# Moving tiles in SBUF, and reusing the meta tokens' keys, in a two-request encoder layer on one Trainium2 core

## The chip, the cores and the metric

The kernel runs on one core of a Trainium2 chip, on TensorE (PE), VectorE (DVE), ScalarE (ACT), GpSimd (POOL) and SyncE (SP), which issues most DMAs. The metric is the device time of the one launch in microseconds. A run's time is the median of several executions; the profile is one further execution, and its span runs from the first to the last instruction.

## What is computed

One layer of an encoder is applied to two requests that share weights: a "prompt" of 1024 tokens and a "sample" of 512, both float32, width 1024. Cut to what matters here:

```python
def encoder_layer(x, ...):                       # x: (1, 16 + T, 1024), 16 meta tokens first
    h = rmsnorm(x, g_mix)
    q, k, v, u, gate_na, gate_fn = split(h @ w_in)
    y_na = neighbourhood_attention(q, k, v, rel_bias, meta_bias) @ w_branch_na
    y_fn = fourier_mix(u) @ w_branch_fn          # real part of a 2-D DFT over positions and channels
    x = x + (sigmoid(gate_na) * y_na + sigmoid(gate_fn) * y_fn) @ w_out
    a = relu(rmsnorm(x, g_mlp) @ w_up)
    return x + (a * a) @ w_down

def run_trunk(x, meta_tokens, ...):
    h = concatenate([meta_tokens, x])            # the same 16 rows ahead of either request
    return rmsnorm(encoder_layer(h, ...), g_final)[16:]
```

Each token of a grid 64 wide attends to a window of 8 x 16 neighbours and to the 16 meta tokens. The meta tokens' own keys, values and normalized rows depend on nothing but themselves and the weights, so they are equal in both requests. The Fourier mix runs over all 16 + T positions.

## The kernel before

The sample runs first, then the prompt (`run`, L330). Each goes through the same stages: reading and transposing the normalized tokens into `hT` (L262), values (L291), attention with the K and Q projections inside (L474), the gates (L736) with the folding of positions beside them (L823), the merges, the Fourier stage (L909), the output projection, and the MLP. In the prompt the MLP's up and down products are done by a Strassen scheme (class `Halves`, L1156; up at L1417).

Every product is kept near float32 by three products of float32r halves: an operand is split into a rounded part `hi` (a CAST on ACT, L151 or L132) and the rest `lo` (a subtraction on DVE or POOL, L152 or L133), and `mm3` (L121; the matmul is L128) issues hi x hi, hi x lo and lo x hi. Most matmuls contract 128 rows and write 128 x 512. The K and Q projections have their own matmul lines (L491 to L493).

`hT` is a pair of tiles (hi, lo) of shape [128, 8, T + 16]: eight blocks of 128 channels, each a row of T + 16 positions with the 16 meta positions first (`new_hT`, L471). A row of the sample is 528 floats, one of the prompt 1040. Weights rotate through three names of tiles of 1044 floats, `w_raw`, `w_hi`, `w_lo`, two buffers each (`wtile`, L135).

The keys of two heads at a time are made in chunks of columns (L479): 352, 344 and 344 in the prompt, 264 and 264 in the sample. The first chunk begins with the 16 meta positions, whose keys ACT and DVE copy six times into the first and last "slot" of the tile `k` (L528 to L534); POOL first zeroes gaps there (L516, `k<-zero`). From the second pair of heads on, POOL also sends half of `k` to the other 64 partitions by DMA (L537). POOL prepares the mask tiles `bm` too (L727, L734).

`fold_positions` (L823) uses a symmetry of the DFT: it adds and subtracts position p and its mirror. For each of the eight blocks a step adds hi and lo of both halves (L839, into `a` and `b`), and makes sum and difference (L840 to L842); a second series of eight steps splits the results back into `hT`. In the sample `a` is the tile `gain`, of which there is one buffer (L380), and the kept halves lie in `acc` and `hn` tiles. The eight first steps run beside the gates, pinned behind their products. Beside the same gates `fold_u` (L236) multiplies the channel DFT into weights (PE L246), evicts them through ACT and DVE (L132, L133, as `w_hi` and `w_lo`), and stores them by SP (L254, L255); POOL's queue loads them later (L819). `tables` (L200) builds the bias tables of attention in DRAM at the start of the sample.

Within an engine's queue the instructions run in order; the order comes from the scheduler of the tile framework and from the `behind` and `pinned` contexts (L110, L114). A tile's buffer is written again only after all its readers, DMAs among them, are done.

Of the kernel before, what the change touches and what calls it, by code (L numbers as in the profile page):

```python
# [17 lines left out]
F32 = mybir.dt.float32  # L18
F32R = mybir.dt.float32r
# [19 lines left out]
def half_rows(n):  # L39
    return n // 2 + 1  # L40
# [28 lines left out]
class Layer:  # L69
    def __init__(self, tc, ctx, ins, outs):  # L70
# [9 lines left out]
        self.zero = self.const.tile([128, 8], F32, name="zero")  # L80
        nc.vector.memset(self.zero, 0.0)
        self.sgn = self.const.tile([128, 2], F32, name="sgn")
# [117 lines left out]
    def tables(self, marks):  # L200
# [7 lines left out]
        self.mb = self.const.tile([128, H, 48], F32, name="mb")  # L208
        nc.vector.memset(self.mb, -NEG)
        src = self.ins["meta_bias"]  # L210
        src = bass.AP(src.tensor, src.offset, [[0, 128], [NM, H], [1, NM]])
        with tc.tile_pool(name="tab", bufs=1, side="right", reuse_waits="tile") as p:
            mask = p.tile([128, 112], F32, name="mask")
            win = p.tile([128, 15 * 112], F32, name="win")
            with self.behind(marks):
                nc.sync.dma_start(mask, self.ins["colmask"])
                nc.sync.dma_start(win, self.ins["rel_win"])
            at = 0
            for w in (24, 32):

                g = win[:, 15 * at:15 * (at + 2 * w)].rearrange("p (j r b) -> p j r b", j=2, b=w)
                g4 = p.tile([128, 2, 15, w], F32, name=f"g4{w}")
                nc.vector.memset(g4, -NEG)
                for j in range(2):
                    m = mask[:, None, at + j * w:at + (j + 1) * w].to_broadcast([128, 15, w])
                    nc.vector.tensor_tensor(out=g[:, j], in0=m, in1=g[:, j], op=ALU.subtract)
                    nc.vector.tensor_copy(g4[:, j, 3:11], g[:, j, 3:11])
                for t, d in (("un", g), ("4", g4)):
                    nc.sync.dma_start(self.g[t, w].rearrange("j p x -> p j x"), d.rearrange("p j r b -> p j (r b)"))
                at += 2 * w  # L230
            mt = p.tile([128, H, NM], F32, name="mt")
            with self.behind(marks):
                nc.sync.dma_start(mt, src)
            nc.vector.tensor_scalar(out=self.mb[:, :, 16:32], in0=mt, scalar1=-1.0, scalar2=None, op0=ALU.mult)
# [27 lines left out]
    def read(self, name, T, hT, xts, hns, gain):  # L262
# [6 lines left out]
        for t in range(-1, T // 128):  # L269
# [3 lines left out]
            if t < 0:  # L273
                self.gain(gain, "g_mix")
# [4 lines left out]
            last = (hn, hT, 0 if t < 0 else NM + t * 128, n)  # L279
# [11 lines left out]
    def project_v(self, name, T, hT, p, wv):  # L291
# [12 lines left out]
        for t in range(-1 if meta is None else 0, T // 128):  # L304
            n = NM if t < 0 else 128
            pos = 0 if t < 0 else NM + t * 128
# [23 lines left out]
    def run(self, order):  # L330
        pool = self.pool
        hp, close_hT = self.open("hT_0", "left")
        hT = self.new_hT(hp, order[0][1])
        for i, (name, T) in enumerate(order):
# [5 lines left out]
            if i == 0:  # L340
                with pool("first", "right") as p:
# [11 lines left out]
                    self.tables(marks)  # L353
                    for _ in reading:
                        pass
                    self.project_v(name, T, hT, att, self.wv)
            else:
# [25 lines left out]
            else:  # L383
# [3 lines left out]
                temp = lambda: p.tile([128, (NM + T) // 2], F32, name="half", bufs=3)  # L387
                na = (lambda: p.tile([128, 4, 128], F32, name="raw", bufs=2), lambda: self.pair(p, [128, 4, 128]))
            fold = self.fold_positions(name, T, hT, temp, halves)
            beside = [(fold, 0, 8)]  # L390
            if small:
                wide = lambda: self.pair(fn, [128, 4, 260], "wu", 1)
# [23 lines left out]
            with pool(f"u_{name}", "right") as up:  # L416
                u, cos = self.fourier_channels(up, name, T, hT, wu, ahead)
# [39 lines left out]
            if nxt:  # L457
                hp, close_hT = self.open(f"hT_{i + 1}", "left")
                hT = self.new_hT(hp, nxt[1])
# [11 lines left out]
    def new_hT(self, pool, T, extra=NM):  # L471
# [1265 lines left out]
```

## Time and profile before

| | |
|---|---|
| time, median of 3 runs | 1990.62 us (1989.81 to 1994.64) |
| profiled execution: span | 1984.2 us, 6.4 us under that median |
| PE busy | 1921.9 us, 97% |
| DVE, POOL, ACT busy | 1153.6, 796.9, 741.1 us |
| DMA moved | 357 MB, 180 GB/s over the span |

The time of the profiled execution itself isn't listed apart from its span, so the distance from span to median is used as the work around it. The stages by time in the span, in microseconds: sample attention to about 150, its gates and fold to 234, its output projection and MLP from about 290 to 560, prompt attention to 850, gates to 950, merges, Fourier stage and output projection to about 1200, up to 1510, down to the end.

How to read the rows: a row names line, engine and operation, then the tile written and the tiles read, shapes and type. PE's matmuls overlap, so a single one's duration (near 390 ns for 512 columns) is longer than the interval between two; groups of them give the interval. A bracket holds the idle time of that engine just before, and what ended it.

### The profile page before, as it was taken

To read this page: it belongs to the slowest core of one execution; us is meant where nothing else is said; L and a number is where in the kernel's file an instruction comes from. 1 tells how busy PE (TensorE), PEld (TensorE's weight loads), DVE (VectorE), ACT (ScalarE), POOL (GpSimd) and SP (SyncE) were. 2 spreads that over 40 slices of the span, in tenths; PEclk is the share of its full clock that TensorE was granted. 3 is DMA by queue.
4 is the path that set the end of the run, shared out by engine and by line. 5 is a ranking of instruction groups with operands and counts; after the bars stand their busy time and mean duration, and the time that the engine had idled before them with its cause. 6 is when DMAs were issued, how large, how long until landed. Compare 5 with 4: busy or idle time off the path is not lost.

```text
span 1984.2 us, 26426 instructions
## 1 busy us (share of the span) xinstructions
PE 1921.9 (97%) x9539; PEld 1602.2 (81%) x9539; DVE 1153.6 (58%) x1946; ACT 741.1 (37%) x1316; POOL 796.9 (40%) x656
## 2 busy tenths in 40 slices
PE   7999999999899999999999999999999999999997
PEld 5877787888689888888898877888887888888886
DVE  6773444799515566661327386656566326658668
ACT  3664322444214565642313234333333433323333
POOL 1244534455421232342224226878782333323331
PEclk9999999999999999999999999999999999999999
DMA  6757863588655555463542432544546867668733
GB/s 219 197 139 232 228 182 118 182 257 258 207 165 196 131 139 131 126 221 112 135 140 96 160 97 84 181 170 152 175 151 224 301 234 254 211 223 283 274 102 122
DMA packets 305972, 357.43 MB, mean 180 GB/s; under 512 B 44648, under 2 KB 215400, under 8 KB 305288
## 3 DMA queue, kind: packets, MB, share of 16 engines
q1 hardware_dynamic: 292112, 334.86, 51.9%
q0 software_dynamic: 13728, 20.88, 4.5%
q8 instruction: 75, 1.23, 0.3%
q14 instruction: 57, 0.47, 0.1%
HBM read 262.41 MB, written 95.83 MB: 181 GB/s over the span
## 4 chain that ended last, share of the span: by engine, by line
PE 76%; DVE 9%; DMA 5%; issue 4%; POOL 3%; ACT 2%; SPq 0%; POOLq 0%; DVEq 0%; ACTq 0%
PE ps_mm L128 20%; PE ps_o L128 19%; PE ps_s L128 16%; PE ps_t L128 10%; PE ps_mm L491 2%; PE ps_mm L492 2%; PE ps_mm L493 2%; PE ps_o L633 1%; DMA w_raw<-in_w_in 1%; POOL w_lo L152 1%; PE ps_t L613 1%; DVE st L181 1%; DVE h_lo L152 1%; PE ps_t L193 1%; DMA gain<-in_w_fnB 1%
## 5 line engine op out<-in xcount | busy, mean ns | idle before, releaser
L152 POOL TENSOR_TENSOR w_lo<-w_raw,w_hi 128x1024 fp32r<-128x1024 f32 x72 | 182.3, 2533 | 250.3 <-ACT w_hi L151 206.5
L152 POOL TENSOR_TENSOR w_lo<-raw,w_hi 128x1024 fp32r<-128x1024 f32 (+1 forms) x49 | 101.1, 2067 | 211.5 <-ACT w_hi L151 203.0
L151 ACT CAST w_hi<-w_raw 128x1024 fp32r<-128x1024 f32 x90 | 94.4, 1049 | 176.1 <-PE ps_s L128 57.5
L152 DVE TENSOR_TENSOR h_lo<-long,h_hi 128x1024 fp32r<-128x1024 f32 x54 | 84.5, 1567 | 80.1 <-ACT h_hi L151 80.1
L491 PE MATMUL ps_mm<-hT,w_hi 128*128 128x512 f32 (+3 forms) x320 | 126.1, 394 | 0.0
L492 PE MATMUL ps_mm<-hT,w_hi 128*128 128x512 f32 (+3 forms) x320 | 115.0, 359 | 0.0
L493 PE MATMUL ps_mm<-hT,w_lo 128*128 128x512 f32 (+3 forms) x320 | 114.9, 359 | 0.0
L151 ACT CAST h_hi<-long 128x1024 fp32r<-128x1024 f32 x54 | 56.8, 1052 | 107.8 <-issue 34.9
L152 DVE TENSOR_TENSOR hs_lo<-short,hs_hi 128x512 fp32r<-128x512 f32 x54 | 63.9, 1183 | 38.9 <-ACT hs_hi L151 36.8
L607 ACT ACTIVATE sc<-sc,ast 128x288 f32<-128x288 f32 (+4 forms) x96 | 53.9, 562 | 76.6 <-DVE ast L605 76.4
L1330 POOL TENSOR_TENSOR x<-w_hi,x 128x512 fp32r<-128x512 f32 (+1 forms) x42 | 67.1, 1597 | 24.3 <-ACT x L1333 24.3
L151 ACT CAST w_hi<-raw 128x1024 fp32r<-128x1024 f32 (+1 forms) x49 | 41.0, 840 | 93.6 <-DVE raw L1546 51.3
L633 PEld LDWEIGHTS ps_o<-pt,vb 104*64 104x64 f32 (+6 forms) x576 | 62.1, 164 | 11.3 <-POOL vb L570 4.6
L493 PEld LDWEIGHTS ps_mm<-hT,w_lo 128*128 128x128 f32 x320 | 60.2, 188 | 8.5
L633 PE MATMUL ps_o<-pt,vb 104*64 104x128 f32 (+6 forms) x576 | 63.0, 245 | 3.6 <-POOL vb L570 2.0
L128 PE MATMUL ps_t<-gate,x 128*128 128x512 f32 x264 | 65.3, 396 | 0.0
L128 PE MATMUL ps_mm<-gate,x 128*128 128x512 f32 x256 | 64.3, 395 | 0.0
L570 POOL TENSOR_TENSOR vb<-vr,vb 96x384 fp32r<-96x384 f32 (+4 forms) x48 | 48.7, 1033 | 35.6 <-ACT vb L569 33.6
L727 POOL MEMSET bm<- 64x96 f32 (+2 forms) x64 | 11.2, 175 | 127.4 <-DVE ast L605 99.9
L492 PEld LDWEIGHTS ps_mm<-hT,w_hi 128*128 128x128 f32 x320 | 60.9, 190 | 1.7
L491 PEld LDWEIGHTS ps_mm<-hT,w_hi 128*128 128x128 f32 x320 | 60.8, 190 | 1.7
L605 DVE CUSTOM_DVE_ANT_0 sc<-ps_s,bm 128x288 f32<-128x288 f32 (+4 forms) x96 | 46.4, 483 | 25.0 <-PE ps_s L601 15.3
(699 smaller groups left out, 5607.6 us busy)
## 6 DMA issues: line engine op xcount, KB each, us to landing
w_raw<-in_w_in SPq DMA_DIRECT2D x54, 512.0 KB
long<-hidden_prompt SPq DMA_DIRECT2D x54, 512.0 KB
raw<-in_w_down SPq DMA_DIRECT2D x39, 512.0 KB
w_raw<-in_w_up SPq DMA_DIRECT2D x34, 512.0 KB
hidden_prompt<-h SPq DMA_DIRECT2D x32, 512.0 KB
short<-hidden_sample SPq DMA_DIRECT2D x54, 256.0 KB
w_lo<-in_w_down SPq DMA_DIRECT2D x18, 512.0 KB
w_raw<-in_w_out SPq DMA_DIRECT2D x16, 512.0 KB
```

The source lines that it names most:

```text
L128: self.nc.tensor.matmul(out, a, b, start=(i == 0 and not more), stop=(i == len(terms) - 1), skip_group_check=more)
L151: nc.scalar.copy(out=hi, in_=raw)
L152: (lo_engine or nc.gpsimd).tensor_tensor(out=lo, in0=raw, in1=hi.bitcast(F32), op=ALU.subtract)
L181: nc.vector.scalar_tensor_tensor(out=a, in0=y, scalar=y, in1=v, op0=ALU.mult, op1=ALU.mult)
L491: nc.tensor.matmul(ps, a[0], b[0], start=(kt == 0), stop=False)
L492: nc.tensor.matmul(ps, a[0], b[1], start=False, stop=False)
L493: nc.tensor.matmul(ps, a[1], b[0], start=False, stop=(kt == 7))
L570: nc.gpsimd.tensor_tensor(out=lo, in0=vs, in1=hi.bitcast(F32), op=ALU.subtract)
L605: nc.vector.tensor_tensor_reduce(out=sc[:, :W], in0=ps[:, :W], in1=bm[:, :W], scale=1.0, scalar=3e38, op0=ALU.add, op1=ALU.min, accum_out= ...
L607: nc.scalar.activation(out=sc[:, :W], in_=sc[:, :W], func=AF.Exp, bias=st[:, 0:1], scale=-1.0, accum_out=st[:, 1:2])
L633: nc.tensor.matmul(po[:m, j * 128:(j + 1) * 128], v, x, start=(i == 0), stop=(i == len(ops) - 1))
L1330: self.nc.gpsimd.tensor_tensor(out=to, in0=x, in1=y, op=op)
```

## The change

**Placement.** Small tiles that stood in the constant pool move to a pool `edge` on the right side; `wtile` tiles grow to 1088 floats, the meta bias tile shrinks to 288, the two `wu` tiles get 1040 and 1072, and `half` 576. The sample's `hT` rows become 576 floats long, with the 16 meta positions at column 48 and the tokens from column 64; the prompt's rows hold 1024 tokens and no meta rows. The Fourier stage reads the same memory as rows of T + 16 (`folded`). With this, of 6960 matmuls with 512 columns, of which 3576 had operands at a distance in the partition that is no multiple of 256 bytes, there are 7152, of which 32 do. The tail of the sample's cosines and a scratch output of the norm move into `relu` tiles.

**Meta rows.** In the prompt the meta rows are neither read, normalized, transposed nor projected. The sample stores its meta keys (`kmeta`, 8 DMAs on POOL's queue) and, in each fold step, the 16 folded-in positions (`hmeta`, 8 DMAs on SP from `a`); the prompt loads them (20 DMAs on POOL's queue in place of the CASTs from `zero`; one load on SP and eight DVE copies in its fold). K's chunks are 512 and 512 in the prompt, 272 and 256 in the sample.

**Tables.** The second kind of table is made from the first in place by four POOL memsets and stored after the values are projected; before, DVE built it in tiles of its own.

```diff
-        self.zero = self.const.tile([128, 8], F32, name="zero")
+        edge = ctx.enter_context(tc.tile_pool(name="edge", bufs=1, side="right"))
+        self.zero = edge.tile([128, 48], F32, name="zero")[:, :8]
...
-        t = self.wpool.tile([128, 1044], F32R, name=f"w_{kind}", bufs=2)[:, :n]
+        t = self.wpool.tile([128, 1088], F32R, name=f"w_{kind}", bufs=2)[:, :n]
...
+        def rest():
+            for w, g in made:
+                for r in (slice(0, 3), slice(11, 15)):
+                    nc.gpsimd.memset(g[:, :, r], -NEG)
+                store("4", w, g)
+            close()
+        return rest
...
-        for t in range(-1, T // 128):
+        first = -1 if self.lead else 0
+        for t in range(first, T // 128):
...
-    def new_hT(self, pool, T, extra=NM):
-        return [tuple(pool.tile([128, 8, T + extra], F32R, name=f"hT{i}") for i in range(2))]
+    def new_hT(self, pool, T, lead):
+        apart = T + 64 if lead else T
+        flat = [pool.tile([128, 8 * max(apart, T + NM)], F32R, name=f"hT{i}") for i in range(2)]
+        self.lead = lead
+        view = lambda w: [t[:, :8 * w].rearrange("p (k t) -> p k t", k=8) for t in flat]
+        return [tuple(t[:, :, apart - T - lead:] for t in view(apart))], [tuple(view(T + NM))]
...
-        kch = [(0, 352), (352, 344), (696, 344)] if rows == 16 else [(0, 264), (264, 264)]
+        lead = self.lead
+        kch = [(0, 272), (272, 256)] if lead else [(c, 512) for c in range(0, T, 512)]
...
-                        for s in (0, nslot - 1):
+                        for s in (0, nslot - 1) if lead else ():
                             nc.gpsimd.tensor_copy(k[:, :, s, 16:64].rearrange("p i (g c) -> p i g c", g=2)[:, :, :, 0:8],
                                                   self.zero[:, None, None, 0:8].to_broadcast([128, 2, 2, 8]))
-                m = NM if ci == 0 else 0
-                t0 = 64 + c0 + m - NM
+                    if not lead:
+                        for hh in range(2):
+                            for at in [halves[hh]] if pr else halves:
+                                for s in (0, nslot - 1):
+                                    nc.gpsimd.dma_start(ks[hh][at, :, s], self.kmeta[pr][hh])
+                m = lead if ci == 0 else 0
+                t0 = 64 + c0 + m - lead
...
+                    if lead and ci == len(kch) - 1:
+                        nc.gpsimd.dma_start(self.kmeta[pr][hh], ks[hh][own, :, 0])
...
-            for x, s in ((a, slice(0, M)), (b, slice(M, N))):
+            m = 0 if hm is None else NM
+            if m:
+                nc.vector.tensor_copy(a[:, 0:m], hm[:, kt])
+            for x, s in ((a[:, m:], slice(0, M - m)), (b, slice(M - m, N - m))):
                 nc.vector.tensor_tensor(out=x, in0=hi[:, kt, s].bitcast(F32), in1=lo[:, kt, s].bitcast(F32), op=ALU.add)
+            if not m:
+                nc.sync.dma_start(self.hmeta[kt], a[:, 0:NM])
```

The order of the instructions shows three places. First DVE in the sample's gates, where the fold steps begin with the add into `gain` (one step is five rows, its second add goes to an `acc` tile) and the three-row groups `w_lo<-ps_mm` are the evictions of `fold_u`. Before, from the third fold step on:

```order
L839 TENSOR_TENSOR gain<-hT_81,hT_82 128x264
L840 COPY acc_1957<-gain 128x1
L841 TENSOR_TENSOR acc_1957<-gain,acc_1957 128x263
L842 TENSOR_TENSOR acc_1957<-gain,acc_1957 128x263
L133 TENSOR_TENSOR w_lo<-ps_mm,w_hi 128x256
L839 TENSOR_TENSOR gain<-hT_81,hT_82 128x264
L133 TENSOR_TENSOR w_lo<-ps_mm,w_hi 128x4
L839 TENSOR_TENSOR acc_1958<-hT_81,hT_82 128x264
L840 COPY acc_1958<-gain 128x1
L841 TENSOR_TENSOR acc_1958<-gain,acc_1958 128x263
L133 TENSOR_TENSOR w_lo<-ps_mm,w_hi 128x252
```

and after, from the second fold step on:

```order
L878 TENSOR_TENSOR gain<-hT_93,hT_94 128x264
L881 COPY acc_1972<-gain 128x1
L882 TENSOR_TENSOR acc_1972<-gain,acc_1971 128x263
L883 TENSOR_TENSOR acc_1971<-gain,acc_1971 128x263
L134 TENSOR_TENSOR w_lo<-ps_mm,w_hi 128x256
L878 TENSOR_TENSOR acc_1972<-hT_93,hT_94 128x264
L134 TENSOR_TENSOR w_lo<-ps_mm,w_hi 128x4
L134 TENSOR_TENSOR w_lo<-ps_mm,w_hi 128x252
L878 TENSOR_TENSOR gain<-hT_93,hT_94 128x264
```

The first of the groups moved from behind the third step to behind the second; the next one moved from inside the seventh to behind the fourth, and the last from behind the eighth into the sixth.

Second SP's queue at the same place, where `w_raw` are loads of gate weights and `wu` the stores of `fold_u`. Before:

```order
L145 DMA w_raw<-in_w_in 128x8x128
L254 DMA wu_2003<-w_hi 128x512
L255 DMA wu_2004<-w_lo 128x512
L773 DMA relu<-in_w_na 128x4x128
L145 DMA w_raw<-in_w_in 128x8x128
L254 DMA wu_2003<-w_hi 128x512
L255 DMA wu_2004<-w_lo 128x512
L145 DMA w_raw<-in_w_in 128x8x128
```

and after:

```order
L146 DMA w_raw<-in_w_in 128x8x128
L266 DMA wu_2018<-w_hi 128x512
L267 DMA wu_2019<-w_lo 128x512
L880 DMA hmeta<-gain 128x16 x2
L146 DMA w_raw<-in_w_in 128x8x128
L266 DMA wu_2018<-w_hi 128x512
L267 DMA wu_2019<-w_lo 128x512
L880 DMA hmeta<-gain 128x16 x2
L146 DMA w_raw<-in_w_in 128x8x128
```

The stores of the fold's 16 columns stand in pairs between the stores of `fold_u` and the next load of gate weights, and the load of `relu` went behind them.

Third POOL's queue at the begin of the prompt's attention, where `k` is first the place of a weight's low half and then the keys of the first pair of heads. Before:

```order
L152 TENSOR_TENSOR k<-w_raw,k 128x1024
L516 CAST k<-zero 128x2x2x8 x8
L727 MEMSET bm 64x96
L734 COPY bm<-mb 128x24
L727 MEMSET bm 64x128
```

and after:

```order
L153 TENSOR_TENSOR k<-w_raw,k 128x1024
L550 DMA k<-kmeta_82 64x2x64 x4
L550 DMA k<-kmeta_83 64x2x64 x4
L550 DMA k<-kmeta_84 64x2x64 x2
L550 DMA k<-kmeta_85 64x2x64 x2
L762 MEMSET bm 64x96
L769 COPY bm<-mb 128x24
```

Eight CASTs, for the first two pairs of heads, gave way to twelve loads, ahead of the same mask work.

More of the change, by code (lines that the diff above doesn't have):

```diff
@@ L206, in tables @@
         self.g = {(t, w): self.dram.tile([2, 16 * H, 15 * w], F32, name=f"g_{t}{w}") for t in ("un", "4") for w in (24, 32)}
-        self.mb = self.const.tile([128, H, 48], F32, name="mb")
+        self.mb = self.const.tile([128, 288], F32, name="mb")
         nc.vector.memset(self.mb, -NEG)
+        own = self.mb[:, 16:16 + 32 * H].rearrange("p (h c) -> p h c", c=32)[:, :, 0:NM]
         src = self.ins["meta_bias"]
         src = bass.AP(src.tensor, src.offset, [[0, 128], [NM, H], [1, NM]])
[L212 to L234, printed above, removed]
@@ new lines, in tables @@
+        p, close = self.open("tab", "right")
+        mask = p.tile([128, 112], F32, name="mask")
+        win = p.tile([128, 15 * 112], F32, name="win")
+        with self.behind(marks):
+            nc.sync.dma_start(mask, self.ins["colmask"])
+            nc.sync.dma_start(win, self.ins["rel_win"])
+        at = 0
+        made = []
+        for w in (24, 32):
+            g = win[:, 15 * at:15 * (at + 2 * w)].rearrange("p (j r b) -> p j r b", j=2, b=w)
+            for j in range(2):
+                m = mask[:, None, at + j * w:at + (j + 1) * w].to_broadcast([128, 15, w])
+                nc.vector.tensor_tensor(out=g[:, j], in0=m, in1=g[:, j], op=ALU.subtract)
+            made.append((w, g))
+            at += 2 * w
@@ new lines, in store @@
+        def store(t, w, g):
+            nc.sync.dma_start(self.g[t, w].rearrange("j p x -> p j x"), g.rearrange("p j r b -> p j (r b)"))
+        for w, g in made:
+            store("un", w, g)
+        with self.behind(marks):
+            nc.sync.dma_start(own, src)
+        nc.vector.tensor_scalar(out=own, in0=own, scalar1=-1.0, scalar2=None, op0=ALU.mult)
+        def rest():
+            for w, g in made:
+                for r in (slice(0, 3), slice(11, 15)):
+                    nc.gpsimd.memset(g[:, :, r], -NEG)
+                store("4", w, g)
+            close()
@@ L330, in run @@
     def run(self, order):
+        nc = self.nc
         pool = self.pool
+        self.hmeta = self.dram.tile([8, 128, NM], F32, name="hmeta")
+        self.kmeta = [[self.dram.tile([64, 2, 64], F32R, name=f"kmeta{pr}{hh}") for hh in range(2)] for pr in range(4)]
         hp, close_hT = self.open("hT_0", "left")
-        hT = self.new_hT(hp, order[0][1])
+        hT, folded = self.new_hT(hp, order[0][1], NM)
         for i, (name, T) in enumerate(order):
@@ L351, in run @@
                     w0 = self.qk_weights(0)
[L353 removed]
+                    rest = self.tables(marks)
                     for _ in reading:
@@ L356, in run @@
                     self.project_v(name, T, hT, att, self.wv)
+                    rest()
             else:
@@ L416, in run @@
             with pool(f"u_{name}", "right") as up:
-                u, cos = self.fourier_channels(up, name, T, hT, wu, ahead)
+                u, cos = self.fourier_channels(up, name, T, folded, wu, ahead, (
+                    lambda: mp.tile([128, 512], F32, name="relu", bufs=2).bitcast(F32R)[:, :half_rows(NM + T) + 1]) if small else None)
                 close_hT()
@@ L541, in project @@
                 cs = slice(c * 512, (c + 1) * 512)
-                yield from product(ps, wq, slice(NM + c * 512, NM + (c + 1) * 512))
+                yield from product(ps, wq, slice(lead + c * 512, lead + (c + 1) * 512))
                 for hh in range(2):
@@ L649, in early_gates @@
                     ps = self.psum("mm")
-                    yield from product(ps, w, slice(NM + c * 512, NM + (c + 1) * 512))
+                    yield from product(ps, w, slice(lead + c * 512, lead + (c + 1) * 512))
                     g = p.tile([128, 512], F32, name="ot", tag="ot", bufs=1)
@@ L907, with fourier_channels @@
     LAST = (0, 1, 3, 2)
-    def fourier_channels(self, p, name, T, hT, wu, ahead):
+    def fourier_channels(self, p, name, T, hT, wu, ahead, tails=None):
         hT, = hT
@@ L918, in fourier_channels @@
         un = [p.tile([128, nt, 128], F32R, name=f"un{i}") for i in range(2)]
-        tail = [p.tile([128, 1, R + 1], F32R, name=f"ct{i}") for i in range(2)]
+        tail = [tails().rearrange("p (a b) -> p a b", a=1) if tails else p.tile([128, 1, R + 1], F32R, name=f"ct{i}") for i in range(2)]
         cos = [[None] * nt for _ in range(2)]
@@ L1052, in project_out @@
                     hn = hp.tile([128, D], F32, name="hn", bufs=2)
-                    self.norm(acc[t], gain, hn, junk=p.tile([128, D], BF16, name="junk", bufs=1))
+                    self.norm(acc[t], gain, hn, junk=p.tile([128, 512], F32, name="relu", bufs=2).bitcast(BF16))
                     pending.append((hn, m, t * 128))
```

31 lines of the change are left out of this document (18 added, 13 removed).

## The prediction

> **What bounds the kernel now.** First the page: the share of each engine, PE's row by slices, and the clock.
>
> ```profile
> span 1984.2 us, 26426 instructions
> PE 1921.9 (97%) x9539; PEld 1602.2 (81%) x9539; DVE 1153.6 (58%) x1946; ACT 741.1 (37%) x1316; POOL 796.9 (40%) x656
> PE   7999999999899999999999999999999999999997
> PEclk9999999999999999999999999999999999999999
> ```
>
> TensorE is busy in nearly every slice at the full granted clock, so the time is close to the number of its matmuls times the interval between them. The windows of two stages (prompt's up projection, prompt's gates) show no idle PE at all, each other engine having room:
>
> ```profile
> core 0: us, PE busy (x) PEld busy (x) DVE busy (x) ACT busy (x) POOL busy (x), PEclk, DMA share, GB/s
> 1250.00:1500.00 250.00, 250.00 (x1074) 201.52 (x1073) 152.42 (x143) 85.85 (x131) 196.85 (x126) 1.00 0.46 162
> 850.00:950.00 100.00, 100.00 (x433) 81.03 (x432) 30.52 (x38) 31.39 (x40) 34.13 (x18) 1.00 0.56 171
> ```
>
> So a change has to shorten matmuls, drop some, or touch one of the few places where PE waits. What one matmul costs stands in the chain that ended last, whose pieces are whole groups of 512-column products (start, us, what, count):
>
> ```profile
> 444.19 5.49 PE ps_mm L128 x24
> 449.68 5.44 PE ps_s L128 x24
> ...
> 456.00 5.58 PE ps_o L128 x24
> 461.57 5.51 PE ps_mm L128 x24
> ...
> 850.31 5.55 PE ps_o L128 x24
> 855.86 5.57 PE ps_mm L128 x24
> ...
> 1107.16 5.44 PE ps_o L128 x24
> ...
> 1283.95 2.80 PE ps_t L128 x12
> ```
>
> These do the same work at full clock, yet one product takes 5.44/24 = 226.7 ns in some and 5.58/24 = 232.5 or 2.80/12 = 233.3 ns in others. I computed the operands' addresses from the pools' order and tile sizes. In the groups at 449.68 and 1107.16 the moving and the stationary operand lie a multiple of 256 bytes apart in every matmul. At 456.00 the distances leave 96 and 64 bytes, at 1283.95 they leave 224. At 461.57 sixteen matmuls are at a multiple and eight are off by 160, and the group stands between: (5.51 - 5.44)/8 = 9 ns for each that is off. At 850.31 and 855.86 an operand is hT, whose eight rows step through all remainders, one in eight being a multiple; they average 5.56/24 = 231.7 ns. The groups by form, over many more matmuls, agree: the first form below is off throughout, the second on throughout, and its mean is 7 ns shorter (count, then busy us, mean ns, idle before).
>
> ```profile
> L128 PE MATMUL ps_t<-gate,x 128*128 128x512 f32 x264 | 65.3, 396 | 0.0
> L128 PE MATMUL ps_t<-w_hi,h_hi 128*128 128x512 f32 x128 | 49.8, 389 | 0.0
> ```
>
> The Trainium skill's page "TensorE: Matmul & The Clock Gate" (section "Step-by-step: what each phase is for") says that TensorE reads SBUF through two independent ports, one of them for loading weights; by it the distance between the operands could not matter, and the sum below would be -2.8 us, not -24.9. The alternation inside one stage, 5.44, 5.58, 5.51 us, speaks against that here.
>
> **The change part by part.** *Placement.* Of 6960 matmuls with 512 columns, counted in the program, 1752 use hT and 2048 others lie off a multiple. After the change 32 are off. The 2048 go from 233.3 to 226.7 ns: 2048 x 6.6 = 13.5 us, two thirds of it in the prompt's up projection. The hT products, mixed with their on-multiple neighbours, go from 231.7 to 226.7: 1752 x 5.0 = 8.8 us. Less 32 x 6.6 = 0.2, that is -22.1 us. All of it lies on the path, PE being the limit. Products of 252 to 352 columns I give nothing.
>
> *Keys of the prompt.* The prompt's K product loses its 16 meta columns: four times 24 matmuls in each of three chunks (352, 344, 344 columns) become four times 24 in each of two chunks of 512. Here is one K product's begin, the begin of the Q product behind it, and the meta rows' eight transposes:
>
> ```profile
> 600.30 0.32 PE L491 MATMUL ps_o<-hT,k 128*128 128x352 f32 x1
> 611.70 0.40 PE L491 MATMUL ps_o<-hT,q 128*128 128x512 f32 x1
> 395.79 0.67 PE L193 MATMUL ps_t<-ident,r 16*128 16x16 f32 x8
> ```
>
> K takes 611.70 - 600.30 = 11.40 us, four times 45.6. After: 192 x 226.7 ns = 43.5. That is -2.1 us; the transposes give -0.7.
>
> *Copying instead of computing, on POOL.* In the sample eight stores of meta keys, and in the prompt twenty loads of them, enter POOL's queue; the loads replace 16 CASTs. The rows: a key DMA's issue, four of the CASTs, with POOL's idle time before them in brackets, POOL's next work, and in the sample the last meta key made, and the first reader of a mask whose copies now stand behind two of the stores.
>
> ```profile
> L537 POOL DMA_DIRECT2D k<-k x12 | 6.8, 566 | 14.0 <-DVE k L531 6.7 <-DVE ast L608 4.7 <-DVE ast L605 1.1
> 611.85 0.67 POOL L516 CAST k<-zero 128x32 fp32r<-128x32 f32 x4 [41.23 <-PE ps_s L492]
> 624.00 0.17 POOL L727 MEMSET bm<- 64x96 f32 x1 [11.48 <-DVE ast L605]
> 54.69 0.25 DVE L534 TENSOR_TENSOR k<-ps_o,k 64x96 fp32r<-64x96 f32 x1
> 63.19 0.38 DVE L605 CUSTOM_DVE_ANT_0 sc<-ps_s,bm 128x216 f32<-128x216 f32 x1
> ```
>
> The first pair's eight loads cost 8 x 0.57 = 4.5 us and fall into the 41 us that POOL idles ahead of 611.85. A later pair's four cost 2.3 for 0.67 and end about 614, ten microseconds ahead of 624.00. In the sample two stores go out after 54.94 and cost 1.1, so the copies behind them are done by 57, ahead of 63.19. All at 0. Were POOL late for PE there, a later pair would cost 2.3 - 0.67 = 1.6 us, three pairs 5.
>
> *Folded positions: a new wait.* In the sample each of eight fold steps writes the temporary `gain`, which has one buffer, and now stores 16 columns of it on SP. The next step's first add must wait until the store has landed. Behind it on DVE stand the evictions (L133, then L254/L255's stores) of the folded channel weights, which PE's L246 products and ACT's next evictions wait for. The rows: a fold add; the second and third group of evictions; an SP issue; two stores to DRAM in the chain; the load on POOL that waits for the last one, and POOL's weight split behind it, with the products that read it; and PE's wait at L246 now.
>
> ```profile
> 186.85 0.43 DVE L839 TENSOR_TENSOR gain<-hT,hT 128x264 f32<-128x264 f32 x1
> 202.46 0.42 DVE L133 TENSOR_TENSOR w_lo<-ps_mm,w_hi 128x256 fp32r<-128x256 f32 x1
> 207.82 0.42 DVE L133 TENSOR_TENSOR w_lo<-ps_mm,w_hi 128x256 fp32r<-128x256 f32 x1
> 192.05 0.38 SPq L145 DMA_DIRECT2D w_raw<-in_w_in  x1
> 738.81 3.10 DMA gate_prompt<-ot
> 209.51 6.25 DMA wu<-w_lo
> 216.24 0.78 POOL L819 DMA_DIRECT2D wu_hi<-wu  x1 [7.57 <-DMA wu<-w_lo]
> 217.04 2.41 POOL L152 TENSOR_TENSOR w_lo<-w_raw,w_hi 128x1024 fp32r<-128x1024 f32 x1
> 225.94 2.02 PE L128 MATMUL ps_s<-hT,w_lo 128*128 128x512 f32 x8
> PE ps_mm L246 <- DVE w_lo L133: 2.3, 1, 2.3
> ```
>
> A step takes t = 0.43 (add) + 0.38 (issue) + L (landing). The second group stands after four steps in place of six, so it begins at 186.85 + 3t + 1.5 = 188.3 + 3t, the third, inside the sixth step, at 187.3 + 5t. With L = 3.1: t = 3.9, 200.0 and 206.8, both ahead of 202.46 and 207.82, so PE's 2.3 us might go. Behind the third, POOL's split ends 217.04 + 2.41 - 207.82 = 11.6 us after that group's begin, and PE wants it at 225.9. With L = 6.25: t = 7.1, 209.6 and 222.8; the second group is 7 us late, and 222.8 + 11.6 = 234.4 is 8.5 late for PE, much of it the same delay: +9. I take 0, since 16 columns are a thirty-second of either store (512 columns), which puts them nearest the shorter row. Bounds -2.3 and +9.
>
> The rest is off the path and given nothing: table copies that leave DVE, two stores put later, eight 16-column copies in the prompt's fold, junk and tails in another tile.
>
> Sum: -22.1 - 2.1 - 0.7 = -24.9 us. The profiled span of 1984.2 becomes 1959.3; the median of the runs shown, 1990.62, lies 6.4 above the span, so the same offset gives 1965.7, **1966 us**.
>
> **Rivals.** *1, the distance does nothing*: what differs between groups then comes from their stage. Only 2.1 + 0.7 = 2.8 us go: 1987.8, which is within 0.3% (6 us, about what a measurement can tell). The groups of one stage, alternating within 23 us, speak against it. Chance 0.05. The Trainium skill's rule of two independent ports, on the page named above, would have it so.
>
> *2, slower: the fold chain is paced by its stores.* By the terms above POOL's split is done at 187.3 + 5t + 11.6 = 198.9 + 5t, and PE wants it at 225.9. Landing times in the trace reach far:
>
> ```profile
> DMA to landing us min/median/max: 3.9/5.3/15.1
> ```
>
> (The tile view of wu's stores and loads.) With 15.1, t = 15.9 and 198.9 + 79.5 - 225.9 = 52.5 us late: 1965.7 + 52.5 = 2018. It decides when the cost passes 24.9 + 6, from 5t = 57.9, a landing of 10.8. For it: SP's queue is shared with 512 KB loads. Against: eight in a row would have to be as slow as the slowest of those larger ones. Chance 0.04.
>
> *3, another engine takes over in the prompt's up stage.* POOL is busy 196.85 of 250 us, in order. If it or the weights' loads pace the stage, its 1319 off products keep their 8.7 us: 1974.4. Against it: PE shows no idle there, and a 3% shorter stage leaves POOL 81% busy. Chance 0.08.
>
> **How the numbers follow.** The forecast gets the other 0.83. Its range: -2.3 gives 1963.4, and each 6.6 or 5.0 ns may be 0.5 wrong, 3800 x 0.5 = 1.9 us, so 1961; upward the fold's +9 gives 1975, which takes in rival 3. Beyond lie rivals 1 and 2 and a remainder. Faster than 1984.6: forecast and rival 3, 0.91; within: 0.05; slower: 0.04.
>
> **What would show it.** Right: in the prompt's up groups of 12 go from 2.80 to 2.72 us and gates' groups of 24 from 5.56 to 5.44; K of a pair takes 10.9; PE's wait for w_lo at L246 stays at 2.3 or less; POOL stands ready at 624. Wrong: groups that keep 5.56 with all distances at a multiple (rival 1); fold adds more than 8 us apart on DVE with PE waiting at L246 (rival 2); PE waiting for POOL's w_lo or DVE between 1200 and 1500 (rival 3).

## The result and the profile after

| | before | after |
|---|---|---|
| time, median | 1991.45 us (1989.81 to 1994.64, 4 runs) | 1967.56 us (1964.46 to 1968.26, 4 runs) |
| ratio | | 0.9876, 95% interval 0.9856 to 0.9896 |
| span of the profiled execution | 1984.2 us | 1966.5 us |

The change made the kernel 24 us faster, where 24.9 were forecast, and the time lies within the range. The two profiled spans differ by 17.7 us only; what fills the difference is the subject of the first experiments. (1990.62 us, the starting point of the forecast, is the median of three runs before; the table has a fourth.)

The page of the changed kernel, span, busy shares and clock:

```profile
span 1966.5 us, 26243 instructions
PE 1904.6 (97%) x9435; PEld 1593.8 (81%) x9435; DVE 1150.2 (58%) x1916; ACT 734.7 (37%) x1292; POOL 814.3 (41%) x672
PEclk9999999999999999999999999999999999999999
```

Nothing changed in the kind of limit: PE is busy for 97% as before, and its busy time fell by 17.3 us. The groups in the chain that ended last show where (start, us, what, count). The first pair is the sample's MLP, the second the prompt's gates, the last one the prompt's up stage:

```profile
486.73 5.44 PE ps_s L129 x24
492.17 5.44 PE ps_o L129 x24
...
853.82 5.44 PE ps_mm L129 x24
859.26 5.44 PE ps_s L129 x24
...
1236.89 2.72 PE ps_mm L129 x12
```

That is 226.7 ns a matmul in all three places. Over the whole chain 281 groups of 12 take 2.72 us, where before it were 150, with 111 at 2.80; a few groups beside other waits still take longer. The groups by form say the same for the 264 matmuls whose mean was 396 ns, and leave the form that was already on a multiple as it was:

```profile
L129 PE MATMUL ps_t<-gate,x 128*128 128x512 f32 x264 | 63.7, 390 | 0.0
...
L129 PE MATMUL ps_t<-w_hi,h_hi 128*128 128x512 f32 x128 | 49.8, 389 | 0.0
```

The windows over the prompt's up stage and gates show that no other engine took over:

```profile
core 0: us, PE busy (x) PEld busy (x) DVE busy (x) ACT busy (x) POOL busy (x), PEclk, DMA share, GB/s
1235.00:1485.00 250.00, 250.00 (x1105) 207.07 (x1104) 155.44 (x150) 87.43 (x134) 208.19 (x129) 1.00 0.48 171
840.00:940.00 100.00, 100.00 (x442) 82.79 (x442) 34.24 (x47) 29.92 (x38) 36.64 (x19) 1.00 0.57 175
```

PE does 1105 matmuls in 250 us in place of 1074; POOL is at 208 us of 250 and PE still has no idle time.

The first K product of the prompt, and the Q product behind it, in the timeline of PE:

```profile
597.10 0.39 PE L519 MATMUL ps_o<-hT,k 128*128 128x512 f32 x1
...
607.98 0.39 PE L519 MATMUL ps_s<-hT,q 128*128 128x512 f32 x1
```

That is 10.88 us for 11.40 before. POOL's timeline at the same place, with the loads of the meta keys:

```profile
566.45 4.73 POOL L550 DMA_DIRECT2D k<-kmeta  x8
608.43 2.34 POOL L550 DMA_DIRECT2D k<-kmeta  x4 [37.26 <-issue]
620.20 0.17 POOL L762 MEMSET bm<- 64x96 f32 x1 [9.43 <-DMA bm<-g_un]
```

They cost nearly what was forecast (4.5 and 2.3 us). The later pair's end 9.4 us ahead of POOL's next work, which waits for something else.

The fold of the sample, from DVE's timeline: the first four adds into `gain`; and behind it the wait at L258 (the products of `fold_u`, L246 before) from PE's view of waits:

```profile
190.27 0.42 DVE L878 TENSOR_TENSOR gain<-hT,hT 128x264 f32<-128x264 f32 x1
...
196.53 0.43 DVE L878 TENSOR_TENSOR gain<-hT,hT 128x264 f32<-128x264 f32 x1 [4.22 <-DMA hmeta<-gain]
...
199.48 0.43 DVE L878 TENSOR_TENSOR gain<-hT,hT 128x264 f32<-128x264 f32 x1
...
203.24 0.42 DVE L878 TENSOR_TENSOR gain<-hT,hT 128x264 f32<-128x264 f32 x1
```

```profile
PE ps_mm L258 <- DVE w_lo L134: 1.0, 1, 1.0
```

They begin 6.3, 3.0 and 3.8 us apart (all eight 4.1 on average), where 3.9 was forecast, and PE's wait at this place is 1.0 us in place of 2.3. Only four of the eight adds wait for a store, 9.1 us in sum; the steps between adds that don't wait take 2.9 to 3.8 us.

### The profile page after: what moved, and what is told of

Same layout as the page of the kernel before. It is cut to its first block, busy times and chain, and to the rows that moved or that the text cites. A ratio compares the mean times of both kernels' runs of the same rounds, so it can differ in the third digit from the quotient of the medians.

```text
span 1966.5 us, 26243 instructions
## 1 busy us (share of the span) xinstructions
PE 1904.6 (97%) x9435; PEld 1593.8 (81%) x9435; DVE 1150.2 (58%) x1916; ACT 734.7 (37%) x1292; POOL 814.3 (41%) x672
## 4 chain that ended last, share of the span: by engine, by line
PE 73%; DVE 9%; DMA 8%; issue 4%; POOL 3%; ACT 3%; SPq 0%; POOLq 0%; ACTq 0%; DVEq 0%
PE ps_mm L129 19%; PE ps_o L129 18%; PE ps_s L129 14%; PE ps_t L129 10%; PE ps_mm L519 2%; PE ps_mm L520 2%; PE ps_mm L521 2%; DMA w_raw<-in_w_in 2%; PE ps_o L668 1%; POOL w_lo L153 1%; PE ps_t L648 1%; DMA hmeta<-gain 1%; DVE st L182 1%; DMA w_raw<-in_w_up 1%; ACT w_hi L152 1%
## 5 line engine op out<-in xcount | busy, mean ns | idle before, releaser
L519 PE MATMUL ps_mm<-hT,w_hi 128*128 128x512 f32 (+2 forms) x296 | 121.9, 412 | 0.0
L520 PE MATMUL ps_mm<-hT,w_hi 128*128 128x512 f32 (+2 forms) x296 | 110.6, 374 | 0.0
L521 PE MATMUL ps_mm<-hT,w_lo 128*128 128x512 f32 (+2 forms) x296 | 110.6, 374 | 0.0
L521 PEld LDWEIGHTS ps_mm<-hT,w_lo 128*128 128x128 f32 x296 | 55.8, 189 | 10.5
L134 DVE TENSOR_TENSOR pt<-ps_t,pt 96x384 fp32r<-96x384 f32 (+4 forms) x96 | 52.9, 551 | 9.9 <-ACT pt L133 9.5
L129 PEld LDWEIGHTS ps_t<-gate,x 128*128 128x128 f32 x264 | 49.4, 188 | 10.9 <-DVE r_lo L1484 0.8
```

Of the source, the lines that this page charges most:

```text
L129: self.nc.tensor.matmul(out, a, b, start=(i == 0 and not more), stop=(i == len(terms) - 1), skip_group_check=more)
L134: self.nc.vector.tensor_tensor(out=lo, in0=ps, in1=(hi if ref is None else ref).bitcast(F32), op=ALU.subtract)
L519: nc.tensor.matmul(ps, a[0], b[0], start=(kt == 0), stop=False)
L520: nc.tensor.matmul(ps, a[0], b[1], start=False, stop=False)
L521: nc.tensor.matmul(ps, a[1], b[0], start=False, stop=(kt == 7))
```

## The experiments

All times are medians. The kernels were measured in three groups, each on one chip together with the kernel before. That one took 1990.28 us (14 runs) beside `after_again`, `place_undone`, `meta_undone` and `hmeta_direct`, 1991.37 (7 runs) beside `micro`, `before_again`, `hmeta_slow` and `fold_after`, and 1991.87 (7 runs) beside `fold_after_2` and `after_third`.

**Where the spans' missing 6 us went.** The landmarks of the first pair of profiles, read from PE's timeline, show that the sample gained nothing: its MLP begins 2.7 us later than before. Both kernels were therefore run once more, unaltered, and the changed one a third time.

> The changed kernel once more, unaltered. In its first profile the sample's stages up to the MLP begin 2.7 us later than before (357.84 against 355.17), though the placement should have made them 6 to 7 us earlier. Theory A (chance): the loss comes from what differs between executions, TensorE at half speed for eight matmuls near 15 us (1.6 us) and a load that landed 1.1 us later near 157 us, with half speed behind it (2.4 us in all). Then this profile has the MLP's begin at another time, by more than 1.5 us. Theory B (the change's own new stores and waits in the sample): it begins at 357 to 358.5 again. Either way the time is 1967 us, within 3.

> The kernel before once more, unaltered. If executions differ in the sample's stages by chance, its MLP begins more than 1 us away from 355.17, and the count of 512-column matmuls at half speed behind a stall is not 17 again (3.4 us there; 29 and 35 with 5.8 and 6.9 us in the two profiles of the changed kernel). If the sample's stages are steady for one program, it begins at 355 within 0.5.

> The changed kernel for comparison on the same chip: 1966 to 1968; its profile gives a third sample of the stages that differ between executions: the sample's MLP begins anywhere between 351 and 360, the number of 512-column matmuls at half speed between 17 and 40.

Measured: `after_again` 1967.01 us (1965.69 to 1968.92), span 1963.9; `after_third` 1965.45 us (1962.17 to 1967.89), span 1963.4; `before_again` 1986.21 us with a span of 1984.4. The landmarks, in us from the span's start:

| | before | before_again | after | after_again | after_third |
|---|---|---|---|---|---|
| sample's MLP begins | 355.17 | 356.07 | 357.84 | 352.07 | 353.21 |
| prompt's gates begin | 843.84 | 841.11 | 836.56 | 832.05 | 833.06 |
| last matmul begins | 1970.74 | 1971.01 | 1953.06 | 1950.53 | 1950.00 |
| 512-column matmuls at half speed: extra us | 3.4 | 6.3 | 5.8 | 6.9 | 6.9 |

One program's sample stages differ by up to 5.8 us between executions, so theory A holds for the changed kernel. For the kernel before the answer is less sharp: its two starts of the MLP are 0.90 us apart, between the two bounds that were set, but the time lost at half speed nearly doubles. Chance isn't all of it, either: the three starts after average 354.4 us and the two before 355.6, 1.2 us earlier in place of the 6 to 7 expected. The intervals of the 512-column matmuls ahead of the MLP did shrink, by 3.8 us in sum; half speed took back 1.1 of that on average, and the rest is not explained.

One cause can be seen in PE's timeline of the changed kernel, just behind its first waits:

```profile
17.16 0.63 PE L129 MATMUL ps_s<-w_lo,hT 128*128 128x512 f32 x1
17.59 0.63 PE L129 MATMUL ps_mm<-w_lo,hT 128*16 128x512 f32 x1
18.02 0.63 PE L129 MATMUL ps_mm<-w_hi,hT 128*16 128x512 f32 x1
...
18.87 0.40 PE L129 MATMUL ps_s<-w_hi,hT 128*128 128x512 f32 x1
19.11 0.40 PE L129 MATMUL ps_s<-w_lo,hT 128*128 128x512 f32 x1
```

Matmuls start 427 ns apart until 18.87, then 235. The stretch began at 15.46 and lasted 3.4 us. The Trainium skill, on the page "TensorE: Matmul & The Clock Gate" (section "Part 1: The HAM clock gate (the "warmup" mystery)"), says that the array drops to half its clock after an idle window of about 3.4 us and needs such a window of work to come back, and that the windows run freely; the 427 ns agrees with it, and so do the records of the granted clock: in the profile of the changed kernel half clock is granted, up to the last matmul, for 3.41 or 6.83 us at a time, always at a multiple of 3.41 us from the first record at 18.87, and this grid lies elsewhere in every execution. How long PE must idle does not agree: half clock followed a single idle time of 2.71 us here (at 162.23) and of 1.76 us in the kernel before (at 363.26). The windows from 155 to 175 us, around the first gates, of two executions of the changed kernel (the first profile, then `after_again`) show it in the granted clock too, the third column from the right:

```profile
155.00:175.00 20.00, 17.05 (x78) 13.68 (x77) 1.01 (x3) 8.21 (x15) 6.09 (x4) 0.91 0.69 238
```

```profile
155.00:175.00 20.00, 18.34 (x94) 14.97 (x93) 2.93 (x9) 8.82 (x19) 9.19 (x5) 1.00 0.69 238
```

In the first execution PE was granted 0.91 of its clock there, in the second all of it. The kernel before varies in the same way: its executions were granted 0.987 to 0.994 of the clock in the mean, and took 1995.2 us at 0.987 and 1986.2 at 0.994. Both its profiles happen to be of the fast end (0.993 and 0.994).

This bears on the result too. Fitted within each kernel over 72 executions, 0.001 more of granted clock goes with 1.4 us less. The changed kernel was granted 0.992 on average (12 executions), the kernel before 0.990 (29). Between 0.991 and 0.993 the median of ten executions before is 1988.3 us and of eleven after 1967.0. So at like clock the change is worth about 21 us, and by this estimate some 3 of the measured 24 us come with the clock. Whether the change itself brought the better clock is not shown.

**Is it the distance?**

> The changed kernel with the small tiles, the w tiles and the sample's hT rows at their old sizes; the prompt's keys stay as changed. 3824 of 7152 matmuls with 512 columns are off a multiple of 256 bytes, in place of 32. Theory A (the distance costs 5.0 to 6.6 ns each): 18 to 23 us slower than the changed kernel, 1986 to 1991, and groups of 12 in the prompt's up stage near 2.78 to 2.80 us again. Rival (the interval belongs to the stage, not to the distance): 1967, within 3, groups of 12 stay at 2.72.

```diff
-        self.zero = edge.tile([128, 48], F32, name="zero")[:, :8]
+        self.zero = self.const.tile([128, 8], F32, name="zero")
...
-        t = self.wpool.tile([128, 1088], F32R, name=f"w_{kind}", bufs=2)[:, :n]
+        t = self.wpool.tile([128, 1044], F32R, name=f"w_{kind}", bufs=2)[:, :n]
...
-        apart = T + 64 if lead else T
+        apart = T + lead
```

Measured: 1986.05 us (1981.11 to 1991.51, 10 runs), ratio to before 0.9985 (0.997 to 1.0), where `after_again` on the same chip has 0.9892 (0.9868 to 0.9915). Its up stage, from the chain:

```profile
1300.91 2.80 PE ps_t L128 x12
1303.71 2.80 PE ps_mm L128 x12
```

The old interval is back with these old sizes and nothing else, at a cost of 19.0 us against `after_again`. The intervals of the 512-column matmuls say the same: above 226.7 ns they sum to 24.3 us here and to 4.1 there. The rival is out; that it is the distance, and not something else that the sizes move, is what the next kernel measures by itself.

> A kernel that computes none of the reference, only chains of 48 float32r matmuls from one SBUF tile, each chain with its own distance between moving and stationary operand: 0, 4, 8, 16, 32, 48, 64, 96, 128, 160, 192, 224, 240 bytes beyond a multiple of 512 (da to dm), each chain twice. Theory A (distance): da at 226.7 ns a matmul, 64 to 224 at 231 to 234; both operands moved by 96 together (both) 226.7. With own distance 0 but the next weights 96 bytes away (own), and the reverse (next): if the load of the next weights collides with the running matmul, own is the slow one and next the fast one; if it is the matmul's own pair, the other way round. Rival (stage): all 512-column chains within 0.5 ns of each other. For 256 and 352 columns no difference at any distance (non, nmid, nfar, mon, mmid, mfar), for 448 columns one if the weight load's share decides. Triples of 512 columns with six 128-column matmuls between them (tria on/on, trib small ones off, tric triples off, trid both off): if the small ones' distance spoils the triples, trib is at 231 and tria at 227; if the interruption itself does, tria is at 231 too.

```python
def chain(name, pairs, n=512):
    ps = psp.tile([128, 512], F32, name=name, tag="ps", bufs=4)
    for i, (m, w) in enumerate(pairs):
        nc.tensor.matmul(ps[:, :n], src[:, w:w + 128], src[:, m:m + n], start=(i == 0), stop=(i == len(pairs) - 1))
```

Measured, from the groups by form of `micro` (count, then busy us, mean ns of one):

```profile
L85 PE MATMUL db<-src 128*128 128x512 f32 x96 | 23.1, 399 | 0.0
...
L85 PE MATMUL own<-src 128*128 128x512 f32 x96 | 22.8, 396 | 0.0
...
L85 PE MATMUL dk<-src 128*128 128x512 f32 x96 | 22.7, 395 | 0.0
...
L85 PE MATMUL next<-src 128*128 128x512 f32 x96 | 22.4, 392 | 0.0
...
L85 PE MATMUL both<-src 128*128 128x512 f32 x96 | 22.2, 390 | 0.0
L85 PE MATMUL da<-src 128*128 128x512 f32 x96 | 22.1, 389 | 0.0
...
L85 PE MATMUL non<-src 128*128 128x256 f32 x96 | 11.9, 284 | 0.0
L85 PE MATMUL nmid<-src 128*128 128x256 f32 x96 | 11.8, 282 | 0.0
```

From start to start the means are 226.9 ns at distance 0 and 227.6 with both operands moved; every other distance is slower, 229.0 ns at 64 bytes (where 231 or more was expected), 233.0 at 128 and 233.3 at 192 (`dk`), 236.8 at 4 bytes (`db`), the worst. A further chain, `same`, loads one and the same weights each time, 96 bytes off, and is at 233.6. `own`, whose every matmul is on a multiple itself but runs while weights 96 bytes off are loaded for the next one, is at 234.0; `next`, the reverse, at 229.8. So most of the loss goes with the weights that are loaded for the next matmul, and a smaller part (2.9 ns) with the matmul's own pair. With 256 columns the means are 120.7 on and 119.9 and 118.3 off, with 352 columns 161.1, 162.3 and 160.1: no loss on average. At 448 there is one, 202.7 against 205.3 and 204.3.

The triples with short matmuls between them, by place, again from start to start: with all operands on a multiple (`tria`) the first of three takes 280 ns and the other two 231 each; with all off (`trid`) they take 287, 235 and 232, with the small ones alone off (`trib`) 283, 233 and 232, with the triples alone off (`tric`) 288, 232 and 238. So the interruption itself costs 4 ns on each of the later two, whatever the distances, as the second reading had it. In the attention of the two kernels the distance then hardly shows. Here is one such triple and the short product behind it, before and then after:

```profile
147.31 0.44 PE L491 MATMUL ps_mm<-hT,w_hi 128*128 128x512 f32 x1
147.59 0.39 PE L492 MATMUL ps_mm<-hT,w_hi 128*128 128x512 f32 x1
147.82 0.40 PE L493 MATMUL ps_mm<-hT,w_lo 128*128 128x512 f32 x1
148.05 0.45 PE L633 MATMUL ps_o<-pt,vb 108*128 108x128 f32 x4
```

```profile
148.34 0.45 PE L519 MATMUL ps_mm<-hT,w_hi 128*128 128x512 f32 x1
148.62 0.39 PE L520 MATMUL ps_mm<-hT,w_hi 128*128 128x512 f32 x1
148.85 0.39 PE L521 MATMUL ps_mm<-hT,w_lo 128*128 128x512 f32 x1
149.08 0.46 PE L668 MATMUL ps_o<-pt,vb 108*128 108x128 f32 x4
```

Both take 280, 230 and 230 ns. Over the triples of the prompt with other work on both sides (77 before, 133 after) the three intervals sum to 741.5 ns before and 740.5 after. Why these lose so little to the distance, where `trid` loses 12 ns against `tria`, is open.

**What the meta rows cost and bring.**

> The placement without the rest: the prompt reads, normalizes and projects its meta rows again, with rows of 1040 floats, and no kmeta or hmeta store or load exists. 896 matmuls are off a multiple. Theory A: K 2.1 us, transposes 0.7, and some 640 products of the prompt's gates and values times 5 ns = 3.2 us: 1973 to 1976. If the new stores and waits are what ate the sample's gain (theory B), the sample's MLP begins 4 us or more earlier than in the changed kernel, at 354 or before, and the total is 1968 to 1971; if not, it begins within 2 us of 357.8.

```diff
-                hT, folded = self.new_hT(hp, nxt[1], 0)
+                hT, folded = self.new_hT(hp, nxt[1], NM)
...
-        apart = T + 64 if lead else T
+        apart = T + 64 if T == 512 else T + lead
...
-        kch = [(0, 272), (272, 256)] if lead else [(c, 512) for c in range(0, T, 512)]
+        kch = [(0, 272), (272, 256)] if T == 512 else [(0, 352), (352, 344), (696, 344)]
```

(The stores and loads of kmeta and hmeta are taken out too.) Measured: 1975.57 us (1972.35 to 1980.54), ratio 0.9936 (0.9914 to 0.9958), as theory A had it; the sample's MLP begins at 357.55, no earlier than in the three profiles with the stores (352.07 to 357.84). So these don't eat a gain in sum. The test isn't a clean one, though: without the stores the evictions of `fold_u` stand late again, and PE waits 2.8 us for them at L258. `place_undone` is the other half of it: against before it holds the meta and table changes without the placement, with 248 more matmuls off a multiple. It is 4.2 us faster by the medians, 3.0 by the ratio (0.9985, interval 0 to 6 us), and 2.2 at a granted clock of 0.991 to 0.993 (five executions).

**The fold's wait.**

> The eight stores of the fold steps are replaced by two stores straight from hT, so that no fold step waits for a store; the prompt adds the two parts once. Theory A (the fold's waits of 9.1 us on DVE are hidden, PE waits 1.0 us at L258): 1967, within 1.5, and the fold's adds stand about 2 us apart. Theory B (the waits cost the sample's gates time): 2 to 3 us faster than the changed kernel in the same call, 1964 to 1965.

```diff
-            if not m:
-                nc.sync.dma_start(self.hmeta[kt], a[:, 0:NM])
+            if not m and kt == 0:
+                for i in range(2):
+                    nc.sync.dma_start(self.hmeta[i].rearrange("k p c -> p k c"), hT[i][:, :, 0:NM].bitcast(F32))
```

Measured: 1974.09 us (1969.55 to 1976.37), ratio 0.9924 (0.9898 to 0.995): slower by some 7 us than `after_again`, which neither theory had. The profile is of its fastest execution; in it the stretch from the first gate to the first merge product takes 88.5 us, where the changed kernel's three profiles have 86.6, 83.7 and 83.9. DVE's waits for hmeta are gone, but PE's view of waits in the gates now has two rows that the changed kernel has not, or has at 1.0:

```profile
PE ps_mm L258 <- DVE w_lo L134: 2.8, 1, 2.8
PE ps_mm L129 <- DVE w_lo L134: 2.0, 1, 2.0
```

Without the wait the scheduler puts the evictions of `fold_u` behind the third, inside the seventh and behind the eighth fold step, as in the kernel before; with it, behind the second and fourth and into the sixth. DVE is delayed besides: at 199.34 and 208.17 us an operation of the fold takes 2.6 and 2.5 us in place of 0.43, each while POOL does a weight split (the changed kernel has two such as well, of 2.5 us). The slower executions were also granted less clock (0.988 to 0.990); TensorE is at half speed behind the wait of 2.8 us, at 207.80. The next two kernels test the reading that the place of the evictions is the cause, one with a longer wait, one with the evictions put first by hand and no wait.

> Each fold step also stores all 264 columns of its temporary twice, which makes the wait for the store longer. By the prediction's formula (step t = 0.43 + 3 x 0.38 + L, L about 4.5 to 5 for 132 KB, so t near 6.3; POOL's split at 198.9 + 5t + 3.4 for the later begin here) the split comes 2 to 8 us late for PE, 1969 to 1975. Rival (the scheduler sees the longer wait and puts the evictions ahead of the waiting adds; here they stand inside the second, third and fourth step): nothing of it reaches PE, 1967 within 2, and PE's wait at L258 is 0.5 or less.

```diff
                 nc.sync.dma_start(self.hmeta[kt], a[:, 0:NM])
+                for i in range(2):
+                    nc.sync.dma_start(self.spare[i][kt], a)
```

> As hmeta_direct, with each fold step issued behind the evictions of the step of fold_u that it stands beside, so that the evictions come after one, two and three fold steps, without any wait for a store. If hmeta_direct's 7 us came from evictions that stood behind up to seven fold steps (PE waited 2.0 and 2.8 us there, with TensorE at half speed behind it), this one is at 1965 to 1967.5 and shows no wait at L258 over 0.5; if they came from the two stores or the addition in the prompt, it stays at 1972 to 1975.

```diff
-                with self.pinned():
-                    for steps, first, end in beside:
-                        if first <= done < end:
-                            next(steps)
+                for steps, first, end in beside:
+                    if first <= done < end:
+                        with self.pinned():
+                            next(steps)
```

Measured: `hmeta_slow` 1970.79 us (1969.90 to 1975.84), ratio 0.9896 (0.9877 to 0.9916), not told apart from the changed kernel by its interval; the median lies in the formula's range and not in the rival's. Its profile is of the slowest execution. There the fold steps stand 5.1 to 8.7 us apart, DVE waits 21.7 us for the stores, and the wait at L258 is gone, as the rival had it; but at 237 us, where the last gate's weights are due, PE waits for POOL's split of them, which stands in POOL's queue behind a split that waited 2.7 us for ACT:

```profile
PE ps_o L129 <- POOL w_lo L153: 3.1, 1, 3.1
```

`fold_after` 1964.60 us (1963.30 to 1968.51), ratio 0.987 (0.9851 to 0.9889), 9 us below `hmeta_direct` with the same stores, and the intervals of the two ratios don't meet. Its evictions stand ahead of the first fold step, behind the first and behind the second, and PE's view of waits in the gates has no row for L258 left; the stretch from the first gate to the first merge product takes 82.5 us. So the order of evictions and fold steps was the cause, and the new wait acted through it: it moved the evictions forward.

> fold_after again, beside the changed kernel on one chip. If the evictions' place is worth what PE waited at L258 in the changed kernel (0.5 to 1.0 us in its two profiles, with some half speed behind it), this is 1 to 3 us below after_third: 1964 to 1966. If the first figure of 1964.6 was chance, the two agree within 1 us.

Measured: 1964.68 us (1963.02 to 1965.96), `after_third` beside it 1965.45. The waits agree with the reading (0 against 1.0 us at L258), and from the first gate to the first merge product this profile takes 81.3 us, less than any of the changed kernel's three; but a difference of 0.8 us in the time is not one that these runs can tell. It is the fastest kernel measured, not shown to be faster than the changed one.

## Why the prediction was right, and where it was off

**Placement, -22.1.** The mechanism was right, and this was the term that was sized too large. Undoing it gave 19.0 us. In the traces, the intervals of the 512-column matmuls (those under 250 ns, less 226.7 each) sum to 22.2 us before and 4.0 after: -18.2. By stage: up 8.4 us gained, prompt's gates and the merge behind them 3.7, the sample from its gates to the MLP's end some 4.3 - each near its term. The step that failed is the one on "the hT products, mixed with their on-multiple neighbours": 1752 of them at 5.0 ns. The ones inside attention, interleaved with short matmuls, went only from some 232 ns to 230 or 231: 0.4 us gained in the two attentions, where some 600 of them should have brought 3.0, although all distances are now multiples. `micro` shows the floor: an interrupted run of three doesn't fall below 231 for its later two even with all operands in place. The other 5.0 and the 6.6 ns held.

**Keys, -2.1 and -0.7.** Measured between -2.2 and -4.2 in `place_undone`, with a wide interval; in its trace the time from the first K product of the prompt to the last of the products interleaved with attention falls from 244.1 to 240.0 us. Of the 4.1 us, 2.9 are in these products themselves and 1.2 in the work between them; but `before_again` has 242.9, with 0.4 less in the products and 0.7 less between them, so the second part is not clear of what differs between executions. The term came from the first pair's product, which runs uninterrupted (11.40 to 10.88, as forecast); the other three pairs are interleaved, which may be where the rest comes from.

**kmeta at 0.** Right, in the sample and the prompt, by the cover named: no engine waits for one of these DMAs in a row of the trace.

**The fold's wait at 0.** Right as a sum. The step of 3.9 us matches the mean of 4.1, but partly by luck: only four of the eight adds wait for a store, and the steps go from 2.9 to 6.3 us. And the prediction treated the moved evictions as given beside the wait; the runs show that the wait is what moves them. Both ways without it were measured: evictions left behind the fold steps, +7 us; put ahead, nothing or a small gain. The bound of +9 for slow landings wasn't reached even with two larger stores more in each step (about +4, within the interval): there the scheduler moved the evictions again, and the 3.1 us that reached PE came through POOL's queue, as rival 2 had it, though from another entry of that queue.

**The time.** Of the 6.4 us between span and median, which were taken as the work around the span, only 1.8 are that (1986.21 us for a span of 1984.4); the other 4.6 go with the better clock of the profiled execution. Since only differences went into the forecast, this didn't move it. That the total came out within 1 us is partly luck. At like clock the change is worth about 21 us, 19 of them placement and 2 the rest, where 24.9 were forecast; what brought the measured time nearer is some 3 us of clock, for which the prediction had no term.

**Rivals.** 1 is refuted by `place_undone` and `micro`; the rule of two independent ports (the Trainium skill, "TensorE: Matmul & The Clock Gate", section "Step-by-step: what each phase is for"), by which loading the next weights takes nothing from the running matmul, does not hold for 512 columns here, where a chain with its weights badly placed runs up to 10 ns a matmul slower (236.8 against 226.9). 2 didn't happen: the fold's adds stand at most 6.3 us apart, and PE's wait for the evictions fell. 3 didn't happen either: PE shows no idle time with POOL at 208 of 250 us.

## What to carry to other kernels

Where TensorE is the limit and the chain's groups of equal work take two different times, compare the addresses: tile widths and pool order alone were worth 19 us of 1990 here, for matmuls of 512 columns with weights loaded for each; at 256 and 352 columns `micro` shows nothing to gain. Apply a price taken from uninterrupted groups to uninterrupted groups only, since interleaved work has its own floor. Before a wait is counted as a cost or taken out, look at what the scheduler does with the order around it: a wait of 9 us on DVE was worth having, because it let evictions that TensorE wanted pass ahead. And before a forecast is called exact, compare executions at the same granted clock.

## What the runs showed of the hardware

- A 512-column float32r matmul with a weight load for each starts every 226.9 ns when the operands lie a multiple of 512 bytes apart (in the kernel, of 256), and every 229 to 237 ns at twelve other distances from 4 to 240 bytes; what counts most is the distance to the weights that are loaded meanwhile (234.0 against 229.8 ns). With 256 and 352 columns there is no such loss on average.
- Three such matmuls between short ones take 280, 231 and 231 ns with all operands in place.
- Matmuls ran at 427 ns for up to 5.1 us on end (`hmeta_slow`, at 547 us), at the start of the program and behind stalls of as little as 1.9 us (`before_again`, at 1529 us); the sum was 3.4 to 11.4 us in the profiles of this study and differs between executions of one program. The granted clock of a window misses the first such stretch: at 10 to 30 us it reads 1.00 in the changed kernel, whose first clock record is at 18.87.
- DVE additions and subtractions of 128 x 264 floats took 2.5 to 2.6 us in place of 0.43 where a weight split on POOL ran beside them (`hmeta_direct`).
